# Order of searches, look-ups and the exponential in the expert layers of a two-block kernel

## The chip, the cores and the metric

The kernel runs on one core of a Trainium2 chip. The metric is the device time of one execution in microseconds (us). The engines are TensorE (PE in the rows; its weight loads are PEld), VectorE (DVE), ScalarE (ACT), GpSimd (POOL) and SyncE (SP), which issues the DMAs. Each works through a queue of its own in order and waits on semaphores of the others.

## The reference

Two blocks of two layers each on 256 tokens of width 1024, all in float32. The first block is MLA attention, sparse attention and four gated feed-forward networks. The second block has two layers, each a recurrent mixer followed by an expert layer (`peer_ffn`), and this is the part that matters here:

```python
q = (h @ w_q).reshape(B, S, PEER_HEADS, 2, PEER_DQ // 2)
scores = jnp.einsum('bshpd,hpkd->bshpk', q, sub_keys)
s1, i1 = lax.top_k(scores[..., 0, :], PEER_TOPK)
s2, i2 = lax.top_k(scores[..., 1, :], PEER_TOPK)
cand_s = (s1[..., :, None] + s2[..., None, :]).reshape(..., 256)
top_s, top_pos = lax.top_k(cand_s, PEER_TOPK)
ids = jnp.take_along_axis(cand_id, top_pos, axis=-1)
gate = jax.nn.softmax(top_s, axis=-1)
act = jax.nn.gelu(jnp.einsum('thkd,td->thk', u_tab[idx], hx))
out = jnp.einsum('thk,thkd->td', g * act, v_tab[idx])
```

8 heads each choose the 16 best of 128 x 128 experts for a token: 16 of 128 by either half of the query, then 16 of the 256 sums. `cand_id` is `i1 * 128 + i2`.

## The kernel before, in words

The kernel gathers nothing. It multiplies all 16384 rows of `u` with all tokens, in 128 tiles of 128 experts (`u_tile`), applies gelu, multiplies with a dense matrix of gates, and multiplies the result with all of `v` (`v_operands`, `accumulate_tokens`). Activations lie in `M[128, 128 tiles, 256 tokens]`.

A float32 product is made of three passes with rounded operands: each weight tile is loaded by a DMA into `raw`, ScalarE rounds it into `hi` (line 258), and VectorE or GpSimd subtracts to get `lo` (line 259). TensorE then makes 16 matmuls with `hi` and 8 with `lo` per tile (line 320). `raw`, `hi` and `lo` have three buffers each in this stage. The variable `lo_pat` says which engine makes the `lo` of the next tile: "V" is VectorE, "P" is GpSimd.

The choice of experts runs beside the u tiles. `first_level` (lines 1619 to 1623) finds the 16 best of 128 for 16 half-heads and two halves of the tokens (a = 0, 1) and is issued during the query product ahead of the u tiles. The rest is a list of steps, `todo`, each with a cost. After every u tile a budget grows by 1.7, or by 2.4 while the step at the head of the list is marked "P", and steps are issued while the budget covers the cost of the next. A mark "P" also puts the next tile's `lo` on GpSimd. The steps:
- `second_level(h, a)` (lines 1656 to 1664), 16 of them, marked "P": one add of 128x256, then MAX, MAX_INDEX, MATCH_REPLACE, MAX, MAX_INDEX;
- `begin(a)` (lines 1680 to 1685): the scores minus their maximum into `ws`, which the exponential will read; the numbers of the half-choices as bf16 into `IB`; the found positions split into their two halves, in `HS`;
- `look_up(s, a)` (lines 1690 to 1694): for both halves s of a position, compare `HS` with 0 to 15, multiply by `IB`, and fold the 16 products by adds. Each is a VectorE instruction with two SBUF operands, the first two of 2048 elements;
- `exponents` (line 1697): one ScalarE activation over `ws`, with a table load before and after it, as gelu has another table;
- `weights` (lines 1701 to 1703), `turn` and 64 `gates` steps, which build the dense matrix from one-hot products.

The code order isn't the order of execution: a scheduler arranges the instructions of each engine by its own estimate of when they are ready, and the engines then run the queues it left in strict order.

Of the kernel before, what the change touches and what calls it, by code (L numbers as in the profile page):

```python
# [13 lines left out]
U32 = mybir.dt.uint32  # L14
AF = mybir.ActivationFunctionType
ALU = mybir.AluOpType
# [155 lines left out]
class Kernel:  # L172
# [1299 lines left out]
    def lru(self, l):  # L1472
        nc, tc, A = self.nc, self.tc, self.A
        with self.stream(3, 3), tc.tile_pool(name="lru", bufs=1) as pool:
# [8 lines left out]
            IG = pool.tile([128, 2, KT, T], F32, name="IG")  # L1483
            HS = pool.tile([128, 2, KT, T], F32, name="HS")

            late = pool.tile([128, 3], F32, name="late")

            def zero_after(i, x):
                nc.scalar.activation(late[:, i:i + 1], x, AF.Relu, scale=-1.0)
# [20 lines left out]
            for b in range(4):  # L1510
# [4 lines left out]
                for d in range(2):  # L1515
                    hi, lo = self.wsplit(A["lrug"][b, d], (2, 2, 2, 128))
                    for gt in range(2):
# [7 lines left out]
                        for n in range(2):  # L1525
# [6 lines left out]
                            if gt == 0:  # L1532
                                nc.scalar.activation(HS[:, d, k], R[:, d, k], AF.Tanh, scale=w[:, 4, c:c + 1])
                    k2 = slice(2 * b, 2 * b + 2)
# [22 lines left out]
            for i in range(4):  # L1557
                for d in range(2):
                    x = HS[:, d, 2 * i:2 * i + 2]
                    nc.scalar.activation(x, x, AF.Sqrt, bias=late[:, 1:2])  # L1560
            zero_after(2, HS[:, 1, KT - 1, 0:1])

            def recurrence(i):
                ks = slice(2 * i, 2 * i + 2)
                for d in range(2):
                    nc.vector.tensor_tensor(IG[:, d, ks], IG[:, d, ks], HS[:, d, ks], op=ALU.mult)
                    rv = (lambda x: x[:, ::-1]) if d else (lambda x: x)
                    for k in range(2 * i, 2 * i + 2):
                        nc.vector.tensor_tensor_scan(rv(HS[:, d, k]), rv(R[:, d, k]), rv(IG[:, d, k]), 0.0,
                                                     op0=ALU.mult, op1=ALU.add)  # L1570
# [21 lines left out]
    def peer(self, l):  # L1592
        nc, tc, A = self.nc, self.tc, self.A
        with ExitStack() as st:
# [6 lines left out]
            SI = [tail[:, 512 + a * 256:768 + a * 256].rearrange("p (h j) -> p h j", j=16) for a in range(2)]  # L1601
# [5 lines left out]
            HB = scratch[:, 3840:4096].rearrange("p (s h j) -> p s h j", h=8, j=16)  # L1607
# [32 lines left out]
            for hp in range(16):  # L1640
                p, b = self.product(A["wq"][l, hp], gpool,
                                    (IDX[:, 0, 2 * hp:2 * hp + 2], EQ[:, 1024 + hp % 4 * 256:1280 + hp % 4 * 256]))
# [6 lines left out]
            todo = deque()  # L1649
# [3 lines left out]
            def second_level(h, a):  # L1653
                ca, cb = CA[h % 2], CB[h % 2]
                s1, s2 = SV[a][:, 2 * h], SV[a][:, 2 * h + 1]
                nc.vector.tensor_tensor(ca.rearrange("p (a b) -> p a b", b=16),  # L1656
                                        s1[:, :, None].to_broadcast([128, 16, 16]),
                                        s2[:, None, :].to_broadcast([128, 16, 16]), op=ALU.add)
                t, ix = TOP[a][:, h], POS[a][:, h].bitcast(U32)
                nc.vector.max(t[:, 0:8], ca)  # L1660
                nc.vector.max_index(ix[:, 0:8], t[:, 0:8], ca)
                nc.vector.match_replace(cb, t[:, 0:8], ca, -3e38)
                nc.vector.max(t[:, 8:16], cb)
                nc.vector.max_index(ix[:, 8:16], t[:, 8:16], cb)
# [2 lines left out]

            spare = scratch[:, 4096:4608].bitcast(BF16)
            KK = spare[:, 0:256].rearrange("p (k j) -> p k j", j=16)
            HS = spare[:, 256:512].rearrange("p (s h j) -> p s h j", h=8, j=16)  # L1670
            IB = spare[:, 512:768].rearrange("p (h s j) -> p s h j", s=2, j=16)
            both = EQ.bitcast(BF16)
            EB = both[:, 0:2048].rearrange("p (h k j) -> p h k j", k=16, j=16)
            ws = IDX[:, 2].rearrange("p (h j) -> p h j", j=16)

            def begin(a):
                if a == 0:
                    nc.vector.tensor_copy(KK, self.iota[:, 0:16, None].to_broadcast([128, 16, 16]))
                pos = POS[a].bitcast(U32)
                nc.vector.tensor_tensor(ws[:, 8 * a:8 * a + 8], TOP[a], TOP[a][:, :, 0:1].to_broadcast([128, 8, 16]),  # L1680
                                        op=ALU.subtract)
                nc.vector.tensor_copy(IB, SI[a].bitcast(U32).rearrange("p (h s) j -> p s h j", s=2))
                nc.vector.tensor_scalar(HB[:, 0].bitcast(U32), pos, 4, None, op0=ALU.logical_shift_right)
                nc.vector.tensor_scalar(HB[:, 1].bitcast(U32), pos, 15, None, op0=ALU.bitwise_and)
                nc.vector.tensor_copy(HS, HB.bitcast(U32))

            def look_up(s, a):
                tt = nc.vector.tensor_tensor
                all_ = [128, 8, 16, 16]
                tt(EB, HS[:, s, :, None, :].to_broadcast(all_), KK[:, None].to_broadcast(all_), op=ALU.is_equal)  # L1690
                tt(EB, EB, IB[:, s, :, :, None].to_broadcast(all_), op=ALU.mult)
                for n in (8, 4, 2):
                    tt(EB[:, :, :n], EB[:, :, :n], EB[:, :, n:2 * n], op=ALU.add)
                tt((TOP[a], POS[a])[s], EB[:, :, 0], EB[:, :, 1], op=ALU.add)

# [30 lines left out]
            def gates(g):  # L1726
                t0 = 4 * g
                ts = slice(t0, t0 + 4)

                oh = gpool.tile([128, 2, 4, 128, 2], BF16, name="oh", tag="oh", bufs=2)  # L1730
                first = gpool.tile([128, 2, 128, 2], BF16, name="first", tag="first", bufs=1)
                pairs = [128, 2, 128, 2]
                for dst, n in ((first, 0), (oh[:, :, 0], 1)):
                    ct = CT[:, n, ts].rearrange("p (q t) -> p q t", t=2)
                    nc.vector.tensor_tensor(dst, iota2[:, None].to_broadcast(pairs),
                                            ct[:, :, None].to_broadcast(pairs), op=ALU.is_equal)
                p = self.ps()
                for q in range(2):
                    nc.vector.tensor_tensor(oh[:, q, 1:], first[:, q, None].to_broadcast([128, 3, 128, 2]),  # L1739
                                            W3[:, :, None, t0 + 2 * q:t0 + 2 * q + 2].to_broadcast([128, 3, 128, 2]),  # L1740
                                            op=ALU.mult)
                    for t in range(2):
                        at = (2 * q + t) * 128
                        for n in range(3):
                            nc.tensor.matmul(p[:, at:at + 128], oh[:, q, 0, :, t], oh[:, q, 1 + n, :, t],  # L1745
                                             start=n == 0, stop=n == 2)
                pv = p.rearrange("p (t i) -> p i t", i=128)
                n = done[0]
                if n:
                    nc.vector.tensor_tensor(M[:, :n, ts], M[:, :n, ts], pv[:, :n], op=ALU.mult)  # L1750
                if n < NEXP:
                    nc.scalar.activation(M[:, n:, ts], pv[:, n:], AF.Copy)  # L1752
                done[1] = t0 + 4
# [13 lines left out]
            def v_operands(i):  # L1767
# [4 lines left out]
                if i == 8:  # L1772
# [6 lines left out]
            second = [[(2.4, lambda h=h, a=a: second_level(h, a), "P") for h in range(8)] for a in range(2)]  # L1779
            turns = [(1.0, lambda a=a: turn(a)) for a in range(2)]  # L1780
            gate = [(2.2, lambda g=g: gates(g)) for g in range(ng)]
            decode = [[(1.6, lambda a=a: begin(a))] + [(4.8, lambda s=s, a=a: look_up(s, a)) for s in range(2)]
                      for a in range(2)]

            decode[1][2:2] = [(0.0, exponents)]
            todo.extend(second[0] + decode[0] + second[1] + decode[1] + [(0.9, weights), (2.4, lambda: None)])
            todo.extend(turns + gate)
            budget = 0.0
            for i in range(NEXP):
# [140 lines left out]
```

## Time and profile before

| | |
|---|---|
| median of 3 runs | 3079.17 us (3076.41 to 3083.0) |
| profiled execution | 3076.87 us, span 3075.1 us |
| PE / PEld busy | 97% / 88% |
| DVE / ACT / POOL busy | 78% / 55% / 7% |
| mean granted clock of TensorE | 0.987 |
| u tiles of the two expert layers | from about 1326 us and from about 2282 us |

The page's shares are means over the whole span. What a change of one stage is worth is read from the timeline of that stage: how long TensorE stands, what it waits for, and what that engine was doing meanwhile. "First" and "second layer" below are the two expert layers; tiles are u tiles, counted from 0.

### The profile page before, as it was taken

The numbers are of one execution on the slowest core, as the hardware profiler recorded it, in microseconds if no ns is written. First come the engines' busy times: TensorE is split into PE (matmuls) and PEld (weight loads), VectorE is DVE, ScalarE is ACT, GpSimd is POOL, SyncE is SP. The second block draws the span as 40 slices with busy tenths as digits, with TensorE's granted clock in tenths as the row PEclk, the third lists the DMA queues.
The fourth block names the chain that finished last, engine by engine and source line by source line (L and its number), as shares of the span: only waits on it lengthen the run. The fifth ranks groups of instructions, "written<-read, shape, count | busy, mean of one in ns | idle before, by whom it ended". The sixth has DMA issues, their size and how long they took to land.

```text
span 3075.1 us, 53494 instructions
## 1 busy us (share of the span) xinstructions
PE 2977.6 (97%) x20280; PEld 2701.0 (88%) x20280; DVE 2391.6 (78%) x4889; ACT 1695.3 (55%) x3072; POOL 200.9 (7%) x98
## 2 busy tenths in 40 slices
PE   9999999999999989998999999999898999999998
PEld 8888888888788879898999988888898999988887
DVE  8876997986689698798889655557999888855555
ACT  7556755655666467544554545556744554454554
POOL 0000000000100000451000000000262000000000
PEclk9999999999999989999999999999999999999999
DMA  8853785984059433344444555555344444455554
GB/s 306 277 172 99 241 297 179 316 273 156 15 190 308 152 123 123 131 153 160 155 152 157 169 195 192 193 195 188 117 165 149 161 158 152 158 191 193 193 194 141
DMA packets 155347, 556.56 MB, mean 181 GB/s; under 512 B 17361, under 2 KB 19153, under 8 KB 154833
## 3 DMA queue, kind: packets, MB, share of 16 engines
q1 hardware_dynamic: 154800, 552.62, 53.9%
q8 instruction: 159, 2.61, 0.3%
q14 instruction: 100, 0.81, 0.1%
q10 hardware_dynamic: 288, 0.52, 0.1%
HBM read 552.02 MB, written 1.05 MB: 180 GB/s over the span
## 4 chain that ended last, share of the span: by engine, by line
PE 83%; DVE 11%; ACT 3%; issue 2%; DMA 1%; POOL 0%; SPq 0%; DVEq 0%; ACTq 0%; POOLq 0%
PE ps_mm L320 25%; PE ps_mm L339 13%; PE ps_ax L1433 8%; PE ps_ax L1432 8%; PE ps_ax L1431 8%; PE ps_mm L342 7%; PE ps_mm L1745 3%; PE ps_ax L320 2%; PE ps_mm L672 1%; DVE lo L259 1%; PE ps_ax L1267 1%; ACT hi L258 1%; DVE M L1656 1%; DVE M L1621 1%; DVE M L1620 1%
## 5 line engine op out<-in xcount | busy, mean ns | idle before, releaser
L258 ACT ACTIVATE hi<-raw 128x1024 fp32r<-128x1024 f32 (+1 forms) x952 | 996.5, 1050 | 959.8 <-PE ps_ax L1432 332.6
L259 DVE TENSOR_TENSOR lo<-raw,hi 128x1024 fp32r<-128x1024 f32 (+2 forms) x890 | 1073.8, 1209 | 526.5 <-ACT hi L258 519.4
L320 PE MATMUL ps_mm<-XX,hi 128*128 128x256 f32 (+1 forms) x5664 | 788.5, 289 | 36.1 <-ACT hi L258 18.9
L320 PEld LDWEIGHTS ps_mm<-XX,hi 128*128 128x128 f32 x5664 | 722.1, 192 | 46.7 <-ACT hi L258 20.0
L320 PE MATMUL ps_mm<-XX,lo 128*128 128x256 f32 (+1 forms) x2832 | 406.0, 283 | 10.2 <-DVE lo L259 10.2
L1433 PE MATMUL ps_ax<-lo,ah 128*128 128x512 f32 x1024 | 398.4, 389 | 0.0
L1432 PE MATMUL ps_ax<-hi,al 128*128 128x512 f32 x1024 | 398.4, 389 | 0.0
L1431 PE MATMUL ps_ax<-hi,ah 128*128 128x512 f32 x1024 | 398.3, 389 | 0.0
L320 PEld LDWEIGHTS ps_mm<-XX,lo 128*128 128x128 f32 x2832 | 367.0, 190 | 12.1 <-DVE lo L259 12.1
L339 PE MATMUL ps_mm<-XX,hi 128*128 128x512 f32 x1216 | 308.8, 395 | 2.9 <-ACT sg L502 1.7
L259 POOL TENSOR_TENSOR lo<-raw,hi 128x1024 fp32r<-128x1024 f32 x66 | 172.4, 2623 | 1356.4 <-ACT hi L258 1351.7
L339 PEld LDWEIGHTS ps_mm<-XX,hi 128*128 128x128 f32 x1216 | 218.3, 189 | 44.2 <-ACT sg L502 2.7
L1433 PEld LDWEIGHTS ps_ax<-lo,ah 128*128 128x128 f32 x1024 | 192.2, 188 | 39.9
L1431 PEld LDWEIGHTS ps_ax<-hi,ah 128*128 128x128 f32 x1024 | 192.2, 188 | 39.9
L1432 PEld LDWEIGHTS ps_ax<-hi,al 128*128 128x128 f32 x1024 | 192.2, 188 | 39.9
L342 PEld LDWEIGHTS ps_mm<-XX,lo 128*128 128x128 f32 x1216 | 163.5, 188 | 18.0 <-DVE lo L259 5.5
L339 PE MATMUL ps_mm<-AHL,hi 128*128 128x512 f32 x704 | 177.7, 392 | 0.0
L342 PE MATMUL ps_mm<-XX,lo 128*128 128x256 f32 x1216 | 169.2, 281 | 1.8 <-DVE lo L259 1.8
L1752 ACT ACTIVATE M<-ps_mm 128x376 f32<-128x376 f32 (+42 forms) x128 | 44.6, 348 | 183.3 <-DVE M L1750 183.3
L339 PEld LDWEIGHTS ps_mm<-AHL,hi 128*128 128x128 f32 x704 | 125.7, 188 | 21.9
L1739 DVE TENSOR_TENSOR oh<-first,W 128x768 bf16<-128x768 bf16 x256 | 130.9, 552 | 0.0
L991 DVE SCALAR_TENSOR_TENSOR raw<-raw,one,cb 128x1024 f32<-128x1024 f32 x96 | 123.0, 1281 | 1.5
(449 smaller groups left out, 3766.1 us busy)
## 6 DMA issues: line engine op xcount, KB each, us to landing
raw<-in_pu_dram SPq DMA_DIRECT2D x256, 512.0 KB, 3.2
raw<-in_pv_dram SPq DMA_DIRECT2D x256, 512.0 KB, 3.2
raw<-in_gu_dram SPq DMA_DIRECT2D x175, 512.0 KB, 4.9
raw<-in_ada_dram SPq DMA_DIRECT2D x96, 512.0 KB, 4.5
raw<-in_down_dram SPq DMA_DIRECT2D x64, 512.0 KB, 4.6
raw<-in_hgin_dram SPq DMA_DIRECT2D x32, 512.0 KB, 3.3
raw<-in_wq_dram SPq DMA_DIRECT2D x32, 512.0 KB, 3.2
raw<-in_down_dram SPq DMA_DIRECT2D x32, 384.0 KB, 3.9
```

Of the source, the lines that this page charges most:

```text
L258: self.nc.scalar.activation(hi, src, AF.Copy)
L259: (eng or self.lo_engine()).tensor_tensor(lo, src, hi, op=ALU.subtract)
L320: mm(out, w[a][:, k], xin[b][:, k0 + k], start=k0 == 0 and at == 0, stop=k0 + n == kt and at == 3 * n - 1)
L339: mm(p.rearrange("p (a t) -> p a t", a=2), hi[:, k], xin[:, k0 + k], start=k0 + k == 0, stop=False, skip_group_check=True)
L342: mm(p[:, :T], lo[:, k], xin[:, k0 + k, 0], start=False, stop=k0 + k == kt - 1, skip_group_check=True)
L991: nc.vector.scalar_tensor_tensor(w, w, tick, cb, op0=ALU.mult, op1=ALU.mult, accum_out=self.MOD[:, l, j:j + 1])
L1431: m(o, xh[:, ts], hi[:, cs], start=t == 0, stop=False)
L1432: m(o, xl[:, ts], hi[:, cs], start=False, stop=False)
L1433: m(o, xh[:, ts], lo[:, cs], start=False, stop=t == n - 1)
L1739: nc.vector.tensor_tensor(oh[:, q, 1:], first[:, q, None].to_broadcast([128, 3, 128, 2]), W3[:, :, None, t0 + 2 * q:t0 + 2 * q + 2].to_bro ...
L1745: nc.tensor.matmul(p[:, at:at + 128], oh[:, q, 0, :, t], oh[:, q, 1 + n, :, t], start=n == 0, stop=n == 2)
L1752: nc.scalar.activation(M[:, n:, ts], pv[:, n:], AF.Copy)
```

## The change

The search steps of both halves of the tokens come first, one after the other, with an empty step of cost 9.6 marked "P" ahead of them (four tiles at 2.4). Then `begin` of both halves, then all four look-ups, then the rest. `HS` and `IB` get a copy per half. `exponents` is put ahead of the last look-up in the list. In `IB` every number stands twice, side by side, and the multiply of the look-up reads pairs. It takes over the place in `EQ` that the query product used. Costs of steps change from 1.6 to 2.0 (`begin`) and from 4.8 to 4.1 (`look_up`).

```diff
-            HS = spare[:, 256:512].rearrange("p (s h j) -> p s h j", h=8, j=16)
-            IB = spare[:, 512:768].rearrange("p (h s j) -> p s h j", s=2, j=16)
+            HS = [spare[:, a * 256 + 256:a * 256 + 512].rearrange("p (s h j) -> p s h j", h=8, j=16) for a in range(2)]
...
+            EB2 = both[:, 0:2048].rearrange("p (m q two) -> p m q two", q=8, two=2)
+            IB = [both[:, a * 512 + 2048:a * 512 + 2560].rearrange("p (s m two) -> p s m two", s=2, two=2)
+                  for a in range(2)]
...
-                nc.vector.tensor_copy(IB, SI[a].bitcast(U32).rearrange("p (h s) j -> p s h j", s=2))
+                numbers = SI[a].bitcast(U32).rearrange("p (h s) j -> p s h j", s=2)
+                for s in range(2):
+                    nc.vector.tensor_copy(IB[a][:, s].rearrange("p (h j) two -> p h j two", j=16),
+                                          numbers[:, s, :, :, None].to_broadcast([128, 8, 16, 2]))
...
-                tt(EB, EB, IB[:, s, :, :, None].to_broadcast(all_), op=ALU.mult)
+                tt(EB2, EB2, IB[a][:, s, :, None, :].to_broadcast([128, 128, 8, 2]), op=ALU.mult)
...
-            decode = [[(1.6, lambda a=a: begin(a))] + [(4.8, lambda s=s, a=a: look_up(s, a)) for s in range(2)]
-                      for a in range(2)]
-
-            decode[1][2:2] = [(0.0, exponents)]
-            todo.extend(second[0] + decode[0] + second[1] + decode[1] + [(0.9, weights), (2.4, lambda: None)])
+
+            todo.append((9.6, lambda: None, "P"))
+            todo.extend(second[0] + second[1] + [(2.0, lambda a=a: begin(a)) for a in range(2)])
+
+            todo.extend([(4.1, lambda s=s, a=a: look_up(s, a)) for a in range(2) for s in range(2)])
+            todo.insert(len(todo) - 1, (0.0, exponents))
+            todo.extend([(0.9, weights), (2.4, lambda: None)])
             todo.extend(turns + gate)
```

The first place is ScalarE's queue around the exponential of the first layer, before. The numbers of `hi` and `ps_mm` tell the tiles: `hi_14959` is tile 14's, and 38 more is the next tile (`hi_15187` is tile 20's); `ps_mm_15070` is tile 17's.

```order
L1760 ACTIVATE M_13691<-ps_mm_15032 128x256
L258 ACTIVATE hi_15187<-raw_15185 128x1024
L1760 ACTIVATE M_13691<-ps_mm_15070 128x256
L1697 ACT_TABLE_LOAD
L1697 ACTIVATE M_13691<-M_13691 128x256
L1760 ACT_TABLE_LOAD
L1760 ACTIVATE M_13691<-ps_mm_15108 128x256
L258 ACTIVATE hi_15225<-raw_15223 128x1024
```

The same place in the changed kernel, where lines 1697 and 1760 have become 1703 and 1766:

```order
L1766 ACTIVATE M_13691<-ps_mm_14804 128x256
L258 ACTIVATE hi_14959<-raw_14957 128x1024
L1766 ACTIVATE M_13691<-ps_mm_14842 128x256
L1703 ACT_TABLE_LOAD
L1703 ACTIVATE M_13691<-M_13691 128x256
L1766 ACT_TABLE_LOAD
L1766 ACTIVATE M_13691<-ps_mm_14880 128x256
L258 ACTIVATE hi_14997<-raw_14995 128x1024
```

The exponential stood behind tile 17's gelu and tile 20's `hi`, and now stands behind tile 11's gelu and tile 14's `hi`. It is the same in the second layer.

The second place is VectorE's queue at the end of the look-ups of the first layer, before: lines 1690 to 1694 are the last look-up, and `lo_15339` is tile 24's.

```order
L1690 TENSOR_TENSOR M_13691<-M_13691 128x2048
L1691 TENSOR_TENSOR M_13691<-M_13691 128x2048
L259 TENSOR_TENSOR lo_15339<-raw_15336,hi_15338 128x1024
L1693 TENSOR_TENSOR M_13691<-M_13691 128x8x128
L1693 TENSOR_TENSOR M_13691<-M_13691 128x8x64
L1693 TENSOR_TENSOR M_13691<-M_13691 128x8x32
L1694 TENSOR_TENSOR M_13691<-M_13691 128x128
L259 TENSOR_TENSOR lo_15371<-raw_15368,hi_15370 128x1024
```

The same place in the changed kernel, with the look-up in lines 1696 to 1700 and tile 21's `lo_15220`:

```order
L1696 TENSOR_TENSOR M_13691<-M_13691 128x2048
L1697 TENSOR_TENSOR M_13691<-M_13691 128x2048
L1699 TENSOR_TENSOR M_13691<-M_13691 128x8x128
L1699 TENSOR_TENSOR M_13691<-M_13691 128x8x64
L1699 TENSOR_TENSOR M_13691<-M_13691 128x8x32
L1700 TENSOR_TENSOR M_13691<-M_13691 128x128
L259 TENSOR_TENSOR lo_15220<-raw_15217,hi_15219 128x1024
L259 TENSOR_TENSOR lo_15259<-raw_15256,hi_15258 128x1024
```

Before, `lo` instructions stood between the pieces of the look-ups; now the four look-ups follow one another (three more such blocks stand ahead of this one), and the first `lo` that VectorE makes of a u tile, tile 21's, stands behind them all. GpSimd makes those of tiles 0 to 20.

## Rows read from the trace of the kernel before

**Rows 1.** Page, busy us (share of the span) xinstructions, by engine
```profile
PE 2977.6 (97%) x20280; PEld 2701.0 (88%) x20280; DVE 2391.6 (78%) x4889; ACT 1695.3 (55%) x3072; POOL 200.9 (7%) x98
```

**Rows 2.** TensorE's waits, 1285 to 1460: waited for: us, times, longest us
```profile
PE ps_mm L320 <- ACT hi L258: 6.9, 1, 6.9
PE ps_mm L320 <- DVE lo L259: 5.7, 2, 3.9
```

**Rows 3.** Timeline, TensorE, first layer: start us, us, instruction, [idle before <-releaser]
```profile
1328.81 2.06 PE L320 MATMUL ps_mm<-XX,hi 128*128 128x256 f32 x16
...
1351.58 2.06 PE L320 MATMUL ps_mm<-XX,hi 128*128 128x256 f32 x16
1357.49 1.77 PE L320 MATMUL ps_mm<-XX,lo 128*128 128x256 f32 x8 [3.85 <-DVE lo L259]
...
1398.43 3.78 PE L320 MATMUL ps_mm<-XX,hi 128*128 128x256 f32 x16 [6.89 <-ACT hi L258]
...
1403.07 2.06 PE L320 MATMUL ps_mm<-XX,hi 128*128 128x256 f32 x16
...
1412.64 1.23 PE L320 MATMUL ps_mm<-XX,lo 128*128 128x256 f32 x8 [1.81 <-DVE lo L259]
1413.70 2.07 PE L320 MATMUL ps_mm<-XX,hi 128*128 128x256 f32 x16
```

**Rows 4.** Timeline, TensorE, second layer: tiles 9 and 25
```profile
2307.89 2.06 PE L320 MATMUL ps_mm<-XX,hi 128*128 128x256 f32 x16
...
2369.07 2.06 PE L320 MATMUL ps_mm<-XX,hi 128*128 128x256 f32 x16
```

**Rows 5.** Timeline, ScalarE, first layer: the exponential
```profile
1395.32 0.42 ACT L1697 ACTIVATE M<-M 128x256 f32<-128x256 f32 x1 [8.85 <-DVE M L1680]
```

**Rows 6.** Timeline, GpSimd: subtractions of the first layer (two rows) and the second
```profile
1343.48 2.39 POOL L259 TENSOR_TENSOR lo<-raw,hi 128x1024 fp32r<-128x1024 f32 x1 [0.45 <-ACT hi L258]
...
1398.45 8.60 POOL L259 TENSOR_TENSOR lo<-raw,hi 128x1024 fp32r<-128x1024 f32 x3 [10.89 <-ACT hi L258]
...
2299.79 2.39 POOL L259 TENSOR_TENSOR lo<-raw,hi 128x1024 fp32r<-128x1024 f32 x1 [0.45 <-ACT hi L258]
```

**Rows 7.** Timeline, VectorE: adds of searches (L1656), a cast, the exponential's operand (L1680)
```profile
1345.72 0.43 DVE L1656 TENSOR_TENSOR M<-M 128x256 f32<-128x256 f32 x1
...
1391.78 0.41 DVE L1656 TENSOR_TENSOR M<-M 128x256 f32<-128x256 f32 x1
...
1393.95 0.28 DVE L1682 CAST M<-M 128x256 bf16<-128x256 uint32 x1
...
1395.01 0.27 DVE L1680 TENSOR_TENSOR M<-M 128x128 f32<-128x128 f32 x1
...
2300.14 2.32 DVE L1656 TENSOR_TENSOR M<-M 128x256 f32<-128x256 f32 x1
...
2305.01 0.41 DVE L1656 TENSOR_TENSOR M<-M 128x256 f32<-128x256 f32 x1
```

**Rows 8.** Timeline, VectorE, first layer: look-ups, beside GpSimd until 1407
```profile
1395.92 1.22 DVE L1690 TENSOR_TENSOR M<-M 128x2048 bf16<-128x2048 bf16 x1
1397.18 2.29 DVE L1691 TENSOR_TENSOR M<-M 128x2048 bf16<-128x2048 bf16 x1
...
1399.71 2.54 DVE L1693 TENSOR_TENSOR M<-M 128x1024 bf16<-128x1024 bf16 x1
...
1402.34 2.46 DVE L1693 TENSOR_TENSOR M<-M 128x512 bf16<-128x512 bf16 x1
1404.72 2.61 DVE L1703 TENSOR_TENSOR M<-M,gst 128x256 f32<-128x256 f32 x1
...
1411.36 1.22 DVE L259 TENSOR_TENSOR lo<-raw,hi 128x1024 fp32r<-128x1024 f32 x1
1412.50 1.47 DVE L1693 TENSOR_TENSOR M<-M 128x1024 bf16<-128x1024 bf16 x3
```

**Rows 9.** Line 1739, VectorE, operand repeated in pairs: ns min/median/max
```profile
L1739 DVE TENSOR_TENSOR oh<-first,W x256: 548/551/560, 1438.5 to 2669.3; 128x768 bf16<-128x768 bf16 x128
```

More of the change, by code (lines that the diff above doesn't have):

```diff
@@ L1681, in begin @@
                                         op=ALU.subtract)
-                nc.vector.tensor_copy(IB, SI[a].bitcast(U32).rearrange("p (h s) j -> p s h j", s=2))
+                numbers = SI[a].bitcast(U32).rearrange("p (h s) j -> p s h j", s=2)
+                for s in range(2):
+                    nc.vector.tensor_copy(IB[a][:, s].rearrange("p (h j) two -> p h j two", j=16),
+                                          numbers[:, s, :, :, None].to_broadcast([128, 8, 16, 2]))
                 nc.vector.tensor_scalar(HB[:, 0].bitcast(U32), pos, 4, None, op0=ALU.logical_shift_right)
                 nc.vector.tensor_scalar(HB[:, 1].bitcast(U32), pos, 15, None, op0=ALU.bitwise_and)
-                nc.vector.tensor_copy(HS, HB.bitcast(U32))
+                nc.vector.tensor_copy(HS[a], HB.bitcast(U32))
             def look_up(s, a):
@@ L1689, in look_up @@
                 all_ = [128, 8, 16, 16]
-                tt(EB, HS[:, s, :, None, :].to_broadcast(all_), KK[:, None].to_broadcast(all_), op=ALU.is_equal)
-                tt(EB, EB, IB[:, s, :, :, None].to_broadcast(all_), op=ALU.mult)
+                tt(EB, HS[a][:, s, :, None, :].to_broadcast(all_), KK[:, None].to_broadcast(all_), op=ALU.is_equal)
+                tt(EB2, EB2, IB[a][:, s, :, None, :].to_broadcast([128, 128, 8, 2]), op=ALU.mult)
                 for n in (8, 4, 2):
```

## The prediction

> **What bounds the kernel now.** I read the page first: TensorE is busy for 97% of the span [rows 1], so a change that adds no matmul can only give back time in which TensorE stands still or runs slowly. Next come the waits of TensorE around the search stage of the first expert layer: one of 6.9 us for ScalarE's `hi`, two of together 5.7 us for VectorE's `lo` [rows 2]. Then TensorE's timeline. From the second u tile (tile 1, 1328.81) to tile 9 (1351.58) a tile takes 22.77/8 = 2.846 us [rows 3]. From tile 9 to tile 25 (1413.70) 62.12 us go by where 16 tiles need 45.54, so 16.6 us are lost, idle times and slow restarts together. In the second layer it is 2369.07 - 2307.89 = 61.18 us, a loss of 15.6 [rows 4]. These 32.2 us are all the change can win, since no other wait touches what it edits. The restart is dear as well as the wait: tile 21, after the longest idle time, takes 4.64 us (1398.43 to 1403.07) instead of 2.85, 1.8 more [rows 3].
>
> Who is late? ScalarE waits 8.85 us before the exponential at 1395.32, for its operand: VectorE's subtraction, which ends just then [rows 5, 7]. Behind the exponential in ScalarE's queue stands the `hi` of tile 21, and behind that TensorE. VectorE is simply late: it is still searching when ScalarE has come to the exponential.
>
> **GpSimd and VectorE shut each other out.** A search's add with two SBUF operands needs 0.41 us [rows 7]. Where it began at 2300.14, while GpSimd's subtraction ran from 2299.79 to 2302.18, it took 2.32 us and ended with it [rows 6, 7]. After the restart at 1398.43 GpSimd's three subtractions and VectorE's three two-operand instructions at 1399.71 (16-bit), 1402.34 and 1404.72 alternate, 2.54 us a pair, and the three 16-bit adds that take 1.47 us together once GpSimd is quiet (1412.50) are among the held kind [rows 6, 8]. The Trainium skill, GPSIMD Engine Reference, section 8 (Key points), says that GpSimd contends with VectorE instructions in a 2-port mode or with two SBUF inputs; the 2.32 us agree. The skill's Advanced Engine Details and Errata, VectorE Performance Modes (Mode Summary), names only the 2-port instructions, which no two-operand instruction is; by that the look-ups would run freely beside GpSimd, and that is the second rival below.
>
> **Part 1: all searches first, four tiles more on GpSimd.** The `lo` of tiles 0 to 20 now go to GpSimd without a break (before: 0 to 8 and 16 to 23). So the 3.85 us wait at tile 9 [rows 3] and its twin in the second layer go: tile 9's `lo` no longer queues behind searches. The matmuls, DMAs and their sizes stay; SP's queue isn't moved past anything. But the idle item delays nothing that VectorE does: its searches stand in its queue back to back as before. What it does is to keep GpSimd running beside them.
>
> Twelve search adds are left at 1345.72, which is the same instant as before. A search alone takes 2.17 us (1391.78 to 1393.95) [rows 7]. Beside GpSimd its add waits for the end of a subtraction, and these come every 2.85 us, at TensorE's pace (1343.48, then 1346.33 and so on) [rows 6]. First layer: add 1 at 1345.72, add 2 freed at 1348.72 by tile 9's subtraction, add 3 at 1351.67, adds 4 to 7 at the ends of tiles 11 to 14: 1354.41, 1357.26, 1360.10, 1362.95. Then GpSimd has nothing (below), and adds 8 to 12 follow at 2.17 us, the last at 1373.80. With its other 2.17 us and about 2.0 us of preparing (eight small instructions where the stretch from 1393.95 to the operand's end had four in 1.33 us [rows 7]), the exponential's operand is there at 1378.0.
>
> **Part 2: the exponential.** It is written later in the program, but on ScalarE it now stands behind tile 11's activation and tile 14's `hi`, where it stood behind 17's and 20's: six tiles earlier. Tile 11's activation follows TensorE's tile 11, which ends at 1351.58 + 3 x 2.846 = 1360.1; so ScalarE reaches the exponential near 1361 and waits 17 us; behind it are tile 15's `hi`, then `lo`, then TensorE. TensorE finishes tile 14 at 1351.58 + 6 x 2.846 = 1368.66. From the exponential's start to TensorE's restart it is 3.1 us (1395.32 to 1398.43) [rows 3, 5]. So TensorE restarts at 1381.1: 12.4 us lost, plus 1.8 of slow restart. Second layer, same rule: add 3 starts at 2305.03 instead of 2305.01, adds 4 to 8 at the ends of tiles 10 to 14, the last of them 2319.26, add 12 at 2327.94, the operand at 2332.1, TensorE at 2335.2 instead of 2307.89 + 17.08 = 2324.97 [rows 4, 7]: 10.2 us plus 1.8. If no add were held at all, the last would start at 1345.72 + 11 x 2.17 = 1369.6 and 2305.01 + 9 x 2.17 = 2324.5, and the losses would be 8.2 and 6.8. I take the held values, because the rows show it for just such adds.
>
> **Part 3: both look-ups prepared together, paired entries.** Preparing takes one cast more per half (one such cast: 0.28 us) [rows 7]; they are counted in the 2.0 us above and the 3.7 below. The four look-ups now stand together ahead of tile 21's `lo`, the first that VectorE makes. Before, three `lo` were put between the pieces of each of the first two look-ups. The multiply over 2048 elements takes 2.29 us with a single entry repeated [rows 8]. Instructions whose repeated operand comes in pairs take 0.55 us for 768 elements [rows 9], 1.47 for 2048. The compare of the same size takes 1.22 [rows 8]. I take 1.25, with 2.29 as the upper end; 1.47 would add 0.9 us a layer.
>
> Counted from TensorE's restart, tile 21's `lo` is needed after one slow tile, five normal ones and 16 of 24 matmuls: 4.64 + 14.23 + 1.90 = 20.8 us. VectorE has until then: the rest of preparing, a compare and a multiply, 3.7 us from the operand on, so 0.6 past the restart. Then GpSimd's six subtractions (tiles 15 to 20, which start as soon as `hi` comes) alternate with six two-operand instructions: 6 x 2.54 = 15.2, and 0.7 more because the sixth is a compare of 1.2 us instead of an add of 0.5. Then alone: that look-up's multiply and adds, 1.25 + 1.5 (three adds) + 0.35 (the last one) = 3.1; two whole look-ups of 1.25 + 1.25 + 1.5 + 0.35 = 4.35; the `lo` itself 1.2. Sum 0.6 + 15.9 + 3.1 + 8.7 + 1.2 = 29.5, which is 8.7 us too late. The same count for the kernel before, from 1399.71 (three pairs, fold, compare, multiply, `lo`), ends at 1412.58, and TensorE's matmul that waits for this `lo` starts at 1412.64 [rows 3, 8], so the way of counting holds. For the restart I take 1.7: the idle times of before in the first layer, 6.9 + 5.7 = 12.6 [rows 2], leave 16.6 - 12.6 = 4.0 for three restarts, 1.8 of it after the longest. The bounds: 0, if nothing is held; 12.9, if the pairs do nothing (four multiplies of 1.04 us more).
>
> The wait comes in each layer, at the same place, as everything in it is counted from the restart. DMA doesn't decide: tile 18's raw load can start when tile 15's `lo` is done, and its `hi` is wanted two tiles later. The 64 gate steps start three tiles later and still end before the last tiles; VectorE is not the bound there. Cost 0.
>
> **Sum.** After: (12.4 + 1.8 + 8.7 + 1.7) + (10.2 + 1.8 + 8.7 + 1.7) = 24.6 + 22.4 = 47.0 us. Before: 32.2. So +14.8 us. The profiled execution took 3076.87 us (span 3075.1), within the three runs of 3076.4 to 3083.0 with median 3079.17; on it that is 3091.7, forecast 3092. Its own range is 3084 (adds not held in the searches: 4.2 + 3.4 less) to 3099.
>
> **Rivals.**
> Pairs do nothing: everything as above, but 4.2 us more per layer: 3100. For it: no row has this shape with 16-bit pairs in a multiply of 2048. Against: the 0.55 us rows, which are multiplies with pairs. 8%.
>
> Look-ups not held: 16-bit instructions run beside GpSimd, so 29.5 becomes 29.5 - 6 x 2.1 = 17, under 20.8, and the second wait is gone. After 12.4 + 10.2 + 3.6 = 26.2, 6.0 us won: 3071. Against: the 2.54 us of a 16-bit add. 11%.
>
> Nothing held, searches included: 8.2 + 6.8 + 3.6 = 18.6, 13.6 won: 3063, faster. It decides once the second wait is gone and the first is under 11.2 us in the mean of both layers (2 x (11.2 + 1.8) = 26.0, 6.2 under 32.2). Against: 2.32 us at 2300.14. 6%.
>
> It does what it says: VectorE is ready before ScalarE comes to the exponential and before tile 21. All 32.2 won: 3045. The operand would have to be ready 17 us sooner. 4%.
>
> The forecast 67%, the rest 4%.
>
> **Chances and range.** A difference of 0.2% is 6.2 us; less can't be told from none. Slower: forecast, pairs and a little of the rest, 0.77. Within: look-ups not held, and the rest, 0.13. Faster: 0.10. Range 3076 to 3101: it holds the forecast's own and the pairs' rival, and ends above the other three, which have 0.21 together.
>
> **What would show it.** Right: no wait of TensorE at tile 9; one of some 12 and 10 us for `hi` at tile 15, with the exponential on ScalarE waiting about 17 us for VectorE's subtraction; one of 8 to 9 us for `lo` at tile 21; adds and compares of 2 to 3 us while GpSimd runs; multiplies of 1.2 to 1.5 us in the look-ups that run alone. Wrong: tile 15 without a wait, look-ups at 1.2 us beside running subtractions, or any idle time of TensorE at the gates.

## The result, and the profile after

The changed kernel takes 3098.64 us (median of 5 runs, 3093.12 to 3100.43), the kernel before 3079.17 (5 runs, 3075.73 to 3083.0): a ratio of 1.0062, 95% interval 1.0051 to 1.0073. It is slower by 19.5 us; 3092 was forecast, in a range of 3076 to 3101. The profiled execution took 3100.17 us with a span of 3098.4, which is 23.3 more than before.

No matmul came or went. TensorE is busy for 4.6 us more, in matmuls that run more slowly; the rest is idle time. The page, as in [rows 1]:

```profile
PE 2982.2 (96%) x20280; PEld 2706.3 (87%) x20280; DVE 2389.9 (77%) x4879; ACT 1695.1 (55%) x3070; POOL 214.9 (7%) x106
```

TensorE's waits in the search stage of the first expert layer (1285 to 1480), then of the second (2300 to 2500), for [rows 2]:

```profile
PE ps_mm L320 <- ACT hi L258: 12.1, 1, 12.1
PE ps_mm L320 <- DVE lo L259: 8.0, 1, 8.0
...
PE ps_mm L320 <- ACT hi L258: 9.9, 1, 9.9
PE ps_mm L320 <- DVE lo L259: 8.7, 1, 8.7
```

And its timeline, first layer, then second, for [rows 3, 4]; columns as there:

```profile
1353.36 2.06 PE L320 MATMUL ps_mm<-XX,hi 128*128 128x256 f32 x16
...
1382.65 3.79 PE L320 MATMUL ps_mm<-XX,hi 128*128 128x256 f32 x16 [12.06 <-ACT hi L258]
1387.52 2.08 PE L320 MATMUL ps_mm<-XX,hi 128*128 128x256 f32 x16
...
1411.86 2.07 PE L320 MATMUL ps_mm<-XX,lo 128*128 128x256 f32 x8 [8.04 <-DVE lo L259]
...
1424.03 2.06 PE L320 MATMUL ps_mm<-XX,hi 128*128 128x256 f32 x16
...
2322.91 2.06 PE L320 MATMUL ps_mm<-XX,hi 128*128 128x256 f32 x16
...
2390.80 1.46 PE L320 MATMUL ps_mm<-XX,hi 128*128 128x256 f32 x11
```

From tile 9 (1353.36) to tile 25 (1424.03) 70.67 us go by, 25.1 more than 16 tiles need; in the second layer 67.89, 22.4 more. The sum is 47.5 where 32.2 were lost before: the two stages cost 15.3 us more. Tile 9 no longer waits; tile 15 waits for `hi`, tile 21 for `lo`.

ScalarE at the exponential, for [rows 5], and GpSimd, for [rows 6]:

```profile
1379.54 0.42 ACT L1703 ACTIVATE M<-M 128x256 f32<-128x256 f32 x1 [15.71 <-DVE M L1683]
1381.27 0.38 ACT L1766 ACTIVATE M<-ps_mm 128x256 f32<-128x256 f32 x1
1381.55 1.05 ACT L258 ACTIVATE hi<-raw 128x1024 fp32r<-128x1024 f32 x1
```

```profile
1362.34 2.40 POOL L259 TENSOR_TENSOR lo<-raw,hi 128x1024 fp32r<-128x1024 f32 x1 [0.43 <-ACT hi L258]
1382.68 15.11 POOL L259 TENSOR_TENSOR lo<-raw,hi 128x1024 fp32r<-128x1024 f32 x6 [17.94 <-ACT hi L258]
```

ScalarE waits 15.7 us with the exponential; tile 15's `hi` follows only at 1381.55, so GpSimd has nothing to do for 17.9 us and then makes six subtractions in a row. VectorE at that time, for [rows 7, 8]:

```profile
1379.22 0.28 DVE L1683 TENSOR_TENSOR M<-M 128x128 f32<-128x128 f32 x1
...
1381.64 1.22 DVE L1697 TENSOR_TENSOR M<-M 128x2048 bf16<-128x2048 bf16 x1
...
1383.11 2.54 DVE L1699 TENSOR_TENSOR M<-M 128x1024 bf16<-128x1024 bf16 x1
...
1393.15 2.38 DVE L1700 TENSOR_TENSOR M<-M 128x128 f32<-128x128 bf16 x1
1395.56 3.31 DVE L1696 TENSOR_TENSOR M<-M 128x2048 bf16<-128x2048 bf16 x1
1398.90 1.23 DVE L1697 TENSOR_TENSOR M<-M 128x2048 bf16<-128x2048 bf16 x1
...
1410.59 3.49 DVE L259 TENSOR_TENSOR lo<-raw,hi 128x1024 fp32r<-128x1024 f32 x3
```

The multiply with pairs (L1697) takes 1.22 us. Six two-operand instructions from 1383.11 on alternate with the six subtractions, and what is left of the look-ups from 1398.90 on runs free. Tile 21's `lo` starts at 1410.59, behind all four.

Not all of the 23.3 us lies here. This table cuts the span of several runs told below, in us: to the first gelu of the first expert layer; from there to its first matmul with `v` (128 u tiles); from its last such matmul to the second layer's first gelu; that layer's 128 tiles; from its last matmul with `v` to the end. The matmuls with `v` are left out: they take 347.5 us a layer in all these runs.

| run | to gelu | tiles, 1st | between | tiles, 2nd | last |
|---|---|---|---|---|---|
| before | 1330.5 | 425.2 | 183.6 | 424.2 | 16.6 |
| before again (e11) | 1332.4 | 425.2 | 183.6 | 424.3 | 16.5 |
| after | 1332.3 | 433.7 | 188.3 | 431.0 | 18.1 |
| after again (e10) | 1333.3 | 433.8 | 188.2 | 431.0 | 18.4 |
| e2 | 1334.3 | 424.4 | 184.6 | 423.4 | 16.6 |
| e3 | 1336.1 | 435.1 | 184.0 | 433.6 | 18.4 |
| e6 | 1331.9 | 408.6 | 183.6 | 408.6 | 16.7 |
| e8 | 1331.6 | 426.1 | 188.6 | 425.2 | 16.5 |

### The profile page after: what moved, and what is told of

It is laid out like the page before. It is cut to its first block, busy times and chain, and to the rows that moved or that the text cites. A ratio compares the mean times of both kernels' runs of the same rounds, so it can differ in the third digit from the quotient of the medians.

```text
span 3098.4 us, 53480 instructions
## 1 busy us (share of the span) xinstructions
PE 2982.2 (96%) x20280; PEld 2706.3 (87%) x20280; DVE 2389.9 (77%) x4879; ACT 1695.1 (55%) x3070; POOL 214.9 (7%) x106
## 4 chain that ended last, share of the span: by engine, by line
PE 82%; DVE 12%; ACT 3%; DMA 1%; issue 1%; SPq 0%; DVEq 0%; ACTq 0%
PE ps_mm L320 26%; PE ps_mm L339 13%; PE ps_ax L1431 7%; PE ps_ax L1433 7%; PE ps_ax L1432 7%; PE ps_mm L342 7%; PE ps_mm L1751 3%; PE ps_ax L320 2%; PE ps_mm L672 1%; DVE M L1656 1%; PE ps_ax L1267 1%; ACT hi L258 1%; DVE M L1699 1%; DVE lo L259 1%; DMA raw<-in_gu_dram 1%
## 5 line engine op out<-in xcount | busy, mean ns | idle before, releaser
L320 PE MATMUL ps_mm<-XX,lo 128*128 128x256 f32 (+1 forms) x2832 | 407.9, 284 | 16.7 <-DVE lo L259 16.7
L320 PEld LDWEIGHTS ps_mm<-XX,lo 128*128 128x128 f32 x2832 | 369.3, 191 | 18.1 <-DVE lo L259 18.1
L259 POOL TENSOR_TENSOR lo<-raw,hi 128x1024 fp32r<-128x1024 f32 x74 | 186.2, 2523 | 1344.3 <-DVE lo L259 818.8
L1758 ACT ACTIVATE M<-ps_mm 128x364 f32<-128x364 f32 (+42 forms) x128 | 43.5, 340 | 184.7 <-DVE M L1756 184.7
```

Source lines behind the costliest of these rows:

```text
L259: (eng or self.lo_engine()).tensor_tensor(lo, src, hi, op=ALU.subtract)
L320: mm(out, w[a][:, k], xin[b][:, k0 + k], start=k0 == 0 and at == 0, stop=k0 + n == kt and at == 3 * n - 1)
```

## The experiments

Diffs are against the changed kernel, unless said. e1 to e4, e5 to e8 and e9 to e11 ran together, each group beside runs of the kernel before.

**e1: no operands for GpSimd.**

```diff
+    zeros = False
...
+        if self.zeros:
+            self.nc.gpsimd.memset(lo.bitcast(F32), 0.0)
+            return
         (eng or self.lo_engine()).tensor_tensor(lo, src, hi, op=ALU.subtract)
...
+                self.zeros = 15 <= i <= 20
                 u_tile(i)
+                self.zeros = False
```

> The changed kernel, but GpSimd's six subtractions for tiles 15 to 20 of both expert layers are replaced by a fill with zeros of the same tile (those six tiles lose their low part; nothing else is left out). A fill has no operand to read. Theory (the look-ups are late because GpSimd's subtractions hold VectorE's two-operand instructions): from 1381.6 on the look-ups run free, 4.35 us each, VectorE is through with them near 1399 instead of 1410.6, tile 21's low part is in time, its waits of 8.0 and 8.7 us and about 2 us of restart each go, the waits of 12.1 and 9.9 us at tile 15 stay: near 3078. Rival (four look-ups standing in one piece ahead of that low part are too long whatever GpSimd does): the waits stay, 3096 to 3101.

Measured: 3076.7 us (10 runs), ratio to before 0.9993 (0.9983 to 1.0003). TensorE's only wait left in the first layer's stage, and VectorE's rows there (line numbers are up to 5 higher in this kernel):

```profile
PE ps_mm L325 <- ACT hi L260: 12.0, 1, 12.0
```

```profile
1381.96 0.68 DVE L1704 TENSOR_TENSOR M<-M 128x1024 bf16<-128x1024 bf16 x1
...
1384.00 1.23 DVE L1701 TENSOR_TENSOR M<-M 128x2048 bf16<-128x2048 bf16 x1
...
1386.52 1.48 DVE L1704 TENSOR_TENSOR M<-M 128x1024 bf16<-128x1024 bf16 x3
...
1396.96 1.22 DVE L264 TENSOR_TENSOR lo<-raw,hi 128x1024 fp32r<-128x1024 f32 x1
```

Three of the six fills run ahead of the look-ups and three beside them. The first of the three beside them:

```profile
1387.12 0.95 POOL L262 MEMSET lo<- 128x1024 f32 x1 [16.59 <-PE ps_mm L325]
```

In the same order of queue, the add of 1024 takes 0.68 us for 2.54, the compare 1.23 for 3.31, and tile 21's `lo` starts at 1396.96 for 1410.59 (the stage as a whole lies 1.2 us earlier). The 8.0 and 8.7 us and their restarts were GpSimd's hold; the rival falls.

**e2: the exponential later.**

```diff
-                nc.scalar.activation(ws, ws, AF.Exp)
+                z = gpool.tile([128, 1], F32, name="zexp", bufs=1)
+                nc.scalar.activation(z, M[:, 17, 0:1], AF.Copy, scale=0.0)
+                nc.scalar.activation(ws, ws, AF.Exp, bias=z)
```

> The changed kernel, but the exponential takes a zero made from tile 17's result as its bias, so it stands on ScalarE behind tile 17's gelu and tile 20's hi and no longer ahead of tile 15's hi. Nothing is left out. Theory 1 (the two waits are two separate losses, as the prediction added them): the 12.1 and 9.9 us at tile 15 and their restarts go, the rest stays: near 3073. Theory 2 (VectorE's queue ahead of tile 21's low part sets the end of the stage, and the wait at tile 15 only shows it early): GpSimd's subtractions run beside the searches instead of beside the look-ups and hold as many instructions there, that low part starts at 1405 to 1411 as before, tile 21 waits 16 to 22 us: 3088 to 3099, middle 3094.

Measured: 3078.68 us (10 runs), ratio 0.9997 (0.9987 to 1.0006), 20 us less than the changed kernel: between the two theories, and neither's number. The waits, first layer, then second:

```profile
PE ps_mm L320 <- DVE lo L259: 14.5, 1, 14.5
...
PE ps_mm L320 <- DVE lo L259: 13.5, 1, 13.5
```

VectorE: the last search adds, the first compare of a look-up, tile 21's `lo`:

```profile
1377.37 1.08 DVE L1656 TENSOR_TENSOR M<-M 128x256 f32<-128x256 f32 x1
1380.21 1.09 DVE L1656 TENSOR_TENSOR M<-M 128x256 f32<-128x256 f32 x1
...
1386.42 1.21 DVE L1696 TENSOR_TENSOR M<-M 128x2048 bf16<-128x2048 bf16 x1
...
1404.86 3.49 DVE L259 TENSOR_TENSOR lo<-raw,hi 128x1024 fp32r<-128x1024 f32 x3
```

The wait at tile 15 is gone, but 20.1 us of waiting became 14.5 and 18.6 became 13.5, not 8: the wait for `lo` grew, as theory 2 has it. Theory 2 missed the size. GpSimd's subtractions now lie beside the searches, where an add is held for 0.67 us (1.08 for 0.41) and all else in a search runs; beside the look-ups nearly every instruction met one, and the same six cost 12.5 us there (1381.64 to 1398.90 in the changed kernel, 1380.49 to 1385.26 for the same piece in e1). Tile 21's `lo` starts 5.7 us earlier than in the changed kernel, though the stage begins 2.0 us later. So the exponential cost by what it moved, more than by its own wait.

**e3: the table without pairs.**

```diff
-                tt(EB2, EB2, IB[a][:, s, :, None, :].to_broadcast([128, 128, 8, 2]), op=ALU.mult)
+                tt(EB, EB, IB[a][:, s].rearrange("p (h j) two -> p h j two", j=16)[:, :, :, 0][:, :, :, None].to_broadcast(all_), op=ALU.mult)
```

> The changed kernel with the look-up's multiply in its old form, the table's entry spread over the last dimension, all else kept. Nothing is left out. Theory: 1.07 us more for each of the eight multiplies that were not held (2.29 for 1.22), four a layer ahead of tile 21's low part, less what then stands behind it: 2.4 to 4.2 us a layer, 3103 to 3107. Rival (paired entries bring nothing, since the multiplies lie beside other work): 3096 to 3101.

Measured: 3103.09 us (4 runs), ratio 1.0073 (1.0056 to 1.009): 4.5 us more than with pairs, at the lower edge, with an interval that overlaps the changed kernel's. The two stages grew by 1.4 and 2.6 us only, as the last look-up's adds now stand behind tile 21's `lo`. In the profile the start came 3.8 us later and the time between the layers was 4.3 us shorter (table), so the whole is no measure of the pairs; the stages are. A free multiply takes 2.29 us again.

**e4: no idle tiles.**

```diff
-            todo.append((9.6, lambda: None, "P"))
```

> The changed kernel without the four idle tiles ahead of the searches: GpSimd has the low parts up to tile 16, VectorE from tile 17 on, between the look-ups; the exponential stands where it stood. Nothing is left out. Theory (GpSimd's hold on the look-ups and the look-ups in one piece make the second wait): the 12.1 and 9.9 us at tile 15 stay, only two of the six subtractions lie beside look-ups, the first low part on VectorE starts near 1393 and tile 17 waits 0 to 3 us, the 8.0 and 8.7 us at tile 21 go: 3078 to 3085. Rival (the idle tiles decide nothing, the searches all ahead of the look-ups do): 3096 to 3101.

Measured: 3078.29 us (10 runs), ratio 1.0 (0.999 to 1.0009). TensorE's waits in the first layer:

```profile
PE ps_mm L320 <- ACT hi L258: 12.0, 1, 12.0
PE ps_mm L320 <- DVE lo L259: 0.3, 1, 0.3
```

As expected: only two adds of a look-up are held (2.55 and 2.44 us), the `lo` of tiles 17 on stand between the look-ups, and the second wait is gone. The four idle tiles alone decided between 3098.6 and 3078.3; 19.5 us of it lie in the two stages.

**e5 and e6: look-ups spread among the tiles.** Both edits for tile 17, in e6 for tile 18:

```diff
-                    nc.vector.tensor_copy(KK, self.iota[:, 0:16, None].to_broadcast([128, 16, 16]))
+                    zk = gpool.tile([128, 1], F32, name="zkk", bufs=1)
+                    nc.scalar.activation(zk, M[:, 17, 0:1], AF.Copy, scale=0.0)
+                    nc.scalar.activation(KK, self.iota[:, 0:16, None].to_broadcast([128, 16, 16]), AF.Identity, bias=zk)
...
-                nc.scalar.activation(ws, ws, AF.Exp)
+                z = gpool.tile([128, 1], F32, name="zexp", bufs=1)
+                nc.scalar.activation(z, M[:, 17, 0:1], AF.Copy, scale=0.0)
+                nc.scalar.activation(ws, ws, AF.Exp, bias=z)
```

> The changed kernel with two edits: the exponential behind tile 17 as in the run of that name, and the comparison numbers of the look-ups written by ScalarE with a bias made from tile 17's result, so that no look-up stands ahead of what is ready by then: tile 21's low part then stands on VectorE's queue behind one comparison, one multiply and one sum, and the following low parts stand among the look-ups. Nothing is left out. Theory (what counts is the VectorE work that stands ahead of a low part when its tile comes up; the total of that work fits into the tiles that follow): VectorE is through with the searches near 1386, tile 21's low part ends near 1391 where TensorE wants it at 1391.5, the waits of 14.5 and 13.5 us that the later exponential alone left go with their restarts: 3046 to 3056. Rival (the stage's VectorE work is too much, and what is not waited for at tile 21 is waited for at tiles 22 to 30): 3070 to 3080.

> As the run before, with tile 18 for tile 17 in both edits: tile 21's low part stands ahead of the first look-up on VectorE's queue, and the rest follows later. Nothing is left out. Theory: tile 21's low part ends near 1387.5, 4 us ahead of need, no wait in the stage: 3045 to 3052; the exponential's wait on ScalarE stays away too. Rival (the look-ups and with them the turns and the gates come so late that TensorE pays at the end of the layer): 3060 to 3080.

Measured: e5 3047.32 us (4 runs), ratio 0.9904 (0.9887 to 0.992); e6 3046.66 (4 runs), 0.99 (0.9883 to 0.9916). Each is in its theory's range, and both beat both kernels. There is no wait of TensorE in either stage. A stretch of 90 us in the first layer, before, after and in e6 (us, then busy time and instructions of PE, PEld, DVE, ACT, POOL, then granted clock, DMA share, GB/s):

```profile
1333.00:1423.00 90.00, 77.45 (x621) 76.83 (x621) 86.39 (x246) 35.92 (x53) 33.40 (x13) 0.94 0.44 148
```

```profile
1333.00:1423.00 90.00, 69.91 (x550) 69.49 (x549) 84.10 (x253) 33.00 (x49) 41.93 (x18) 0.87 0.41 132
```

```profile
1333.00:1423.00 90.00, 90.00 (x761) 90.00 (x760) 85.16 (x260) 45.65 (x70) 40.87 (x18) 1.00 0.57 187
```

VectorE is as busy in all three; what differs is what it does first. In e6 tile 21's `lo` starts at 1384.31, behind the searches and ahead of the look-ups, and the next ones stand between their pieces:

```profile
1384.31 1.22 DVE L259 TENSOR_TENSOR lo<-raw,hi 128x1024 fp32r<-128x1024 f32 x1
1385.44 1.22 DVE L1698 TENSOR_TENSOR M<-M 128x2048 bf16<-128x2048 bf16 x1
1386.70 1.23 DVE L1699 TENSOR_TENSOR M<-M 128x2048 bf16<-128x2048 bf16 x1
...
1388.17 1.22 DVE L259 TENSOR_TENSOR lo<-raw,hi 128x1024 fp32r<-128x1024 f32 x1
```

**e7: the edits of e2 and e4 together.**

> The changed kernel with both earlier edits: no idle tiles and the exponential behind tile 17. Nothing is left out. Theory (VectorE's queue sets the end): tile 17's low part is the first on VectorE and stands behind all searches, the first look-up and half the second, near 1390.6 where TensorE wants it at 1380; one wait of 9 to 13 us a layer takes the place of the 12.0 and 9.9 us at tile 15: 3073 to 3080. Rival (gains add up: the 12.0 and 9.9 us at tile 15 and about 2 us of restart each go from the 3078 of the run without idle tiles): 3050 to 3056.

Measured: 3071.02 us (10 runs), ratio 0.9977 (0.9967 to 0.9986), 2 us under the theory's range. The one wait of the first layer; 9.4 us in the second:

```profile
PE ps_mm L320 <- DVE lo L259: 11.5, 1, 11.5
```

The two gains of 20 us against the changed kernel do not add up (28 together): with the exponential out of the way, tile 17 waits for the `lo` that stands behind a look-up and a half.

**e8: pairs alone**, against the kernel before: `IB` with every number twice, and the multiply with pairs (the line that e3 takes out).

> The kernel before with one part of the change, the look-up table with paired entries; searches and look-ups stay in their old order, the exponential in its old place. Nothing is left out. Theory: 1.07 us less for each of the four multiplies of a layer, 0.2 us more for the table's second copy, all of it in VectorE's queue ahead of the low parts that TensorE waits for: 2 to 4 us a layer, 3071 to 3075. Rival (the look-ups of the first half lie beside tiles that wait for nothing, so only the two of the second half count): 3075 to 3077. No effect would be 3077 to 3081.

Measured: 3081.77 us (10 runs), ratio 1.001 (1.0001 to 1.002). No expectation held. TensorE's waits in the first layer, for [rows 2]:

```profile
PE ps_mm L320 <- DVE lo L259: 6.8, 3, 3.7
PE ps_mm L320 <- ACT hi L258: 4.1, 1, 4.1
```

The wait for `hi` fell from 6.9 to 4.1 us, that for `lo` rose from 5.7 in two places to 6.8 in three, with one more restart: in VectorE's queue a search's add (at 1368.35) now stands ahead of two `lo` instructions that it stood behind, and the last look-up's adds ahead of one (tile 24's). The stages grew by 0.9 and 1.0 us. 5.0 more lie between the layers (table).

**e9: e6 without pairs**, with e3's line.

> The kernel of the tile 18 run, with the multiply in its old form without pairs. Nothing is left out. Theory (VectorE now has time to spare between the low parts, so 4 x 1.07 us more a layer are not waited for): 3045 to 3050, no wait of TensorE in tiles 9 to 40. Rival (the low parts among the look-ups come just in time, so each longer multiply is waited for): 2 to 4 us a layer, 3051 to 3055.

Measured: 3045.85 us (4 runs), ratio 0.9897 (0.9881 to 0.9914): the pairs bring nothing once VectorE has time to spare. Its 90 us, still without a wait of TensorE:

```profile
1333.00:1423.00 90.00, 90.00 (x761) 90.00 (x761) 88.26 (x261) 45.34 (x69) 41.07 (x18) 1.00 0.55 180
```

**e10, e11: both kernels again**, unchanged.

> The changed kernel as it is, once more, for what the expert stages do not explain (about 8 of the 23 us between the two profiled executions). Nothing is left out. Theory (one of the eight products at the head of the second expert layer met a GpSimd subtraction by chance): the wait of 12.0 and 8.0 us, 9.9 and 8.7 us return to 0.5 us, the stage from the last product of the first expert layer to the second layer's first gelu is 183.6 to 185.2 us if no product of these took 2.6 us, and near 188.4 if one did. Rival (the change itself lengthens that stage): 188 with no such product.

> The kernel before as it is, once more, for the same question. Nothing is left out. Theory: first gelu of the first expert layer at 1330 to 1336, the stage between the layers 183.6 to 185.2 or near 188.4 as above, both expert stages within 0.5 us of 425.2 and 424.2. Rival: start and middle come out as in the first execution, 1330.5 and 183.6, and only the changed kernel ever shows others.

Measured: 3101.5 and 3078.79 us (one run each). The eight products at the head of the second expert layer, on VectorE (ns min/median/max, first and last start), in e10, then in e11:

```profile
L1083 DVE SCALAR_TENSOR_TENSOR XX<-M,MOD,XX x8: 471/473/2572, 2253.2 to 2258.0; 128x256 fp32r<-128x256 f32 x8
```

```profile
L1083 DVE SCALAR_TENSOR_TENSOR XX<-M,MOD,XX x8: 474/474/475, 2242.5 to 2245.2; 128x256 fp32r<-128x256 f32 x8
```

One of the eight takes 2.57 us, in both profiles of the changed kernel and in e8's, and in none of the other ten. The theory's link holds (188.2 to 188.6 with it, 183.4 to 185.2 without). "By chance" isn't borne out, as it came back, but two profiles can't exclude it. The start of before again, 1332.4, is as e11's theory has it. GpSimd's subtraction beside these products, before, then after:

```profile
2242.24 3.79 POOL L259 TENSOR_TENSOR lo<-raw,hi 128x1024 fp32r<-128x1024 f32 x1 [3.12 <-ACT hi L258]
```

```profile
2253.84 2.56 POOL L259 TENSOR_TENSOR lo<-raw,hi 128x1024 fp32r<-128x1024 f32 x1 [2.71 <-ACT hi L258]
```

It starts 1.7 us after the first product in all thirteen profiles. In ten it takes 3.8 us, and 2.3 of them lie behind the last product: there GpSimd is the one that is held. In the other three it takes 2.6 us, and a product is held.

## Why the prediction was nearly right, step by step

**Tile 9's wait goes:** right.

**The exponential, 12.4 and 10.2 us at tile 15:** measured 12.06 and 9.88; ScalarE waited 15.7 where "about 17" stood. What e2 adds is that this term isn't a loss of its own: without it, 5.6 and 5.1 us of waiting and a restart go, and the rest comes back at tile 21. The sum came out because both terms were counted in the same run, from the same restart.

**The look-ups, 8.7 us at tile 21:** measured 8.04 and 8.68. Its cause, six alternations with GpSimd, is shown by e1. The Trainium skill, GPSIMD Engine Reference, section 8 (Key points), says that VectorE instructions with two SBUF inputs contend with GpSimd; the 2.54 us agree for subtractions, not for e1's fills, beside which (1387.12 to 1388.07) VectorE's adds kept their 1.48 us. The prediction's other rule, by which the look-ups would run free, falls by the 2.54 us too, and with it the rival at 3071.

**Restarts, 1.8 and 1.7:** tile 15 took 4.87 us for 2.85, 2.0 more, and 1.4 in the second layer. At tile 21 what is left of the loss is 3.0 and 2.4, so the 1.7 was too small. All terms together: 47.5 measured, 47.0 predicted. That it is so close is partly luck: the four waits came out 1.3 us shorter (38.7 for 40.0), the restarts 1.8 longer (8.8 for 7.0).

**Pairs, 1.25 us a multiply:** 1.22. Their worth of 4.2 us a layer was too much: 1.4 and 2.6 by e3.

**What failed is the step "on it that is 3091.7":** that the rest of the program takes what it took, since "no other wait touches what it edits". 8.0 of the 23.3 us between the two profiles lie outside the two stages: 1.8 ahead of the first, 4.7 between them, 1.5 at the end.
- The start comes and goes: it lies at 1330.5 to 1336.1 us over thirteen profiles, with before again at 1332.4.
- The 4.7 us between the layers were there in both profiles of the changed kernel. 3.4 of them are the held product: TensorE waits 2.8 us there instead of 1.1, and the matmuls behind run more slowly; 20 us there (2250 to 2270) have a granted clock of 0.91, and 1.00 at the same place before (2240 to 2260). The other 1.3 are lost further ahead, in matmuls of lines 299 to 301: from 2148 to 2152 the granted clock is 0.57, at the same place before (2138 to 2141) 1.00, though the waits ahead of them are as long as before. Between the layers no instruction differs, nor their order on any engine, and GpSimd's subtraction meets the products in every profile. Why a product is held in this kernel and in e8, and GpSimd in the others, is open, and so is the 1.3.
- The 1.5 us at the end belong to the changed kernel as well (18.1 and 18.4, for 16.6 and 16.5): ScalarE's queue takes longer to issue the last output DMAs, before, then after:

```profile
3069.87 1.49 ACTq L1820 DMA_DIRECT2D out_dram<-X  x2
```

```profile
3091.88 2.97 ACTq L1828 DMA_DIRECT2D out_dram<-X  x2
```

It is 2.97 to 3.25 us in the five profiles with 3070 ScalarE instructions (after, e10, e1, e3, e4) and 1.49 in the eight with 3072 or 3076. Why is open.

15.3 + 4.7 + 1.5 = 21.5 in the profiles; the medians differ by 19.5, and the interval of the ratio leaves 15.7 to 22.5. The unprofiled executions can't be divided in this way. The sum was also put on the profiled 3076.87 us, which is 2.3 under the median of before: of the 7.0 us by which the result lies above 3091.7, 2.3 are this base, and nearly all of the other 4.7 is the rest of the program.

The rival that it does what it says (3045, 4%) failed for the reason given, the operand's time; e5 and e6 reach its price by moving other work, not the operand.

## What to carry to other kernels

When an engine works through its queue in order, ask what stands ahead of the instruction that the bottleneck wants next, not how long all of its work is: nearly the same VectorE work cost 47 us (after) or nothing (e6). A wait that is removed gives back only what doesn't come due at the next wait, so try edits together, and count a faster instruction only where it stands ahead of an awaited one. Where GpSimd and VectorE's two-operand instructions hold each other, as here, let GpSimd's work lie beside VectorE instructions with one operand, as e2 did with the searches.

## What the runs showed of the hardware

- A GpSimd fill with zeros of 128x1024 takes 0.95 us and held nothing on VectorE (e1); the subtraction of the same size takes 2.40 alone and 2.52 in alternation, and an add of 0.41 us beside it takes up to 2.32.
- Either engine can be the one that is held: a subtraction that came up 1.7 us after the first of eight products took 3.79 us and let them pass (before), or took 2.56 us and held one of them for 2.1 (after).
- A hold of 2.1 us on one product cost 3.4 us of the whole: the wait, and the slower matmuls behind it.
- An exponential with a bias that is a zero made from another result is a cheap way to place an instruction: 0.2 us for the zero, and 0.51 us for 0.42 with the bias.
